# Operand tiles placed at one remainder of 256 bytes, three of them without meta columns, and weight rows of 1088 bytes

## The chip, the cores and the metric

The kernel runs on one core of one Trainium2 chip. The metric is the device time of one execution in microseconds (us). Three runs of the kernel before gave 1002.52, 1004.66 and 1006.24 us; the median is 1004.66.

## The reference

One layer of a hybrid decoder: 1024 tokens and 16 learned meta tokens ahead of them, model width 1024, float32. The normalised input goes through one wide projection whose columns feed four branches (causal pooling, latent attention with 8 heads, a Conformer convolution, a short gated convolution) and their gates; the branches are projected back, gated, added and projected once more.

```python
h = rms_norm(h_res, pre_norm_g[i])
z = h @ w_in[i]
(pv, pg, cq, ckv, kr, mg, cu, cg, sbcx, sg, gl) = split_cols(z)
...
y_b = (mla_attention(cq, ckv, kr, ...) * jax.nn.silu(mg)) @ w_out_mla[i]
...
gts = jax.nn.sigmoid(gl + gate_bias[i]).reshape(b_, l_, N_BRANCH, D_MODEL)
m = (gts[:, :, 0] * y_a + gts[:, :, 1] * y_b + gts[:, :, 2] * y_c + gts[:, :, 3] * y_d)
h_res = h_res + rms_norm(m @ w_o[i], post_norm_g[i])
...
return h_res[:, N_META:]
```

The meta tokens are dropped from the output. Their columns are needed only where later tokens look back: in the keys and values of the attention, and in the causal convolutions and pooling.

## The kernel before

**Precision.** A float32 operand is split into a high part and a rest ("hi" and "lo", `split`), and each product is three matmuls per block of 128 along the contraction: hi x hi, hi x lo, lo x hi.

**First stage, the projection.** The tokens are cut into two halves of 512 and the weights into 2x2 blocks, and a Strassen-Winograd scheme makes each 2x2 block product from seven products. The seven token operands B11, T2, T1, T3, B21, T4, B22 live in the pool `hb` at the upper end of SBUF (line 514). Each is `[128, 2, 4, n]`: the hi and the lo part, four blocks of the contraction, n columns. n is 512, or 528 with the 16 meta columns behind (`LH`), or 544 for T1 and T2; T3 and B22 have no meta columns. The seven weight blocks A11, S2, S1, S3, A12, A22, S4 are made by `prep` and `blk` in the pool `wp`, which lies behind the pools `const` and `tp` at the lower end. Each is `[128, 2, 4, 128]`, 4096 bytes a partition, from seven buffers of one tag that go round.

`unit` runs the seven products: A11 with B11, S2 with T2, S1 with T1, S3 with T3, A12 with B21, A22 with T4, S4 with B22. In the first of the pairs A12 comes right behind A11. `product` runs one of them, 12 matmuls: for each of four k the weights hi with the operand's hi, hi with lo, and lo with hi. The weights are the stationary side, the tokens stream. 23 units run with 512 columns at once; five, whose outputs need the meta tokens, run in two halves of 256 and 272 columns. Two small weight blocks (`kv`, `kr`) go through `plain` first.

The PSUM tiles tell the products apart in the profile: `ps_pa` is A11 and A12, `ps_pb` is S2 and S3, `ps_pc` is S1 and S4, `ps_pd` is A22. Buffer numbers are left out there, so that B11, B21 and B22 are all `B`, and T1 to T4 are all `T`.

**Second stage, attention** (`attend`, `maxima`): keys `kt` `[100, 2, 1040]` for even and odd heads, values `vt` `[128, 9, 192]`, queries `qt` `[100, 2, 512]`; scores `ps_s`, outputs `ps_o`. Between them run the output projections of three branches (`ps_y`).

**Third stage:** the attention's output projection and the last product with `w_o`, again by seven products; here the tokens are stationary and the weights `wa` stream.

**The order of the work.** `Plan` records every operation, and `flush` writes the order of each engine's queue out by hand from costs of its own; `Pool.lay_out` places the buffers. Each pool is a row of tags, each tag a row of equal buffers, rounded up to a multiple of 64 bytes. A buffer whose place an earlier pool held becomes free when that pool's last user ends. All weights, keys and values are loaded by SP's queue.

Of the kernel before, what the change touches and what calls it, by code (L numbers as in the profile page):

```python
# [25 lines left out]
ALU = mybir.AluOpType  # L26
# [10 lines left out]
KH = KD // 2  # L37

SBUF = 212832
H = 8  # L40
QK = 96
EPS = 1e-6
NEG = -1e30

LH = 512 + NM

C_PV, C_PG, C_CQ, C_CKV, C_KR, C_MG = 0, 256, 512, 768, 896, 928
C_CU, C_CG, C_SC, C_SG, C_GL = 1440, 1952, 2208, 2976, 3232
# [8 lines left out]
B11, B21, B22, T1, T2, T3, T4 = range(7)  # L57

B12 = T3

CH_KV = [(0, 512), (512, 512), (1024, 16)]
CH_L = [(0, 348), (348, 346), (694, 346)]
# [83 lines left out]
class Pool:  # L146
# [2 lines left out]

    def __init__(self, plan, pool, bufs=1, psum=False, side="left"):
        self.plan, self.pool, self.bufs, self.psum, self.groups = plan, pool, bufs, psum, {}
        self.space = "psum" if psum else side
        self.base = None
# [21 lines left out]
    def lay_out(self, start):  # L177

        for g in self.groups.values():
            g["one"] = -(-max(b.bytes for b in g["order"]) // 64) * 64  # L180
        size = sum(g["n"] * g["one"] for g in self.groups.values())
        at = start = start - size - SBUF % 64 if self.space == "right" else start
        for tag, g in self.groups.items():
            if not g["slots"]:
                g["slots"] = [{"i": i, "live": None, "after": 0} for i in range(g["n"])]
                for sl in g["slots"]:
                    self.pool.tile([P, g["one"] // 4], F32, tag=f"{tag}_{sl['i']}", name=f"{tag}_{sl['i']}")
            for sl in g["slots"]:
                sl["place"] = (self.space, at, at + g["one"])
                at += g["one"]  # L190
        if self.space == "right" and not self.base:
            self.base = self.pool.tile([P, SBUF % 64 // 4], F32, tag="end", name="end")
        return start if self.space == "right" else at


# [242 lines left out]
def trunk_kernel(ctx, tc, a):  # L438
# [2 lines left out]
    PE, ACT, DVE, POOL, SP = (plan.engine(e) for e in ("PE", "ACT", "DVE", "POOL", "SP"))  # L441
    ctx.enter_context(tc.manual_schedule())

    def pool(stack, **kw):
        return plan.open(stack, Pool(plan, stack.enter_context(tc.tile_pool(bufs=1, **kw)),
                                     psum=kw.get("space") == PSUM,
                                     side="dram" if kw.get("space") == DRAM else kw.get("side", "left")))

# [59 lines left out]


    one = ExitStack()  # L510
    hpool = pool(one, name="hb", side="right", reuse_waits="tile")
    HB = {}
    for b, name in ((B11, "B11"), (T2, "T2"), (T1, "T1"), (T3, "T3"), (B21, "B21"), (T4, "T4"), (B22, "B22")):
        HB[b] = hpool.tile([P, 2, KH, {T3: 512, B22: 512, T1: 544, T2: 544}.get(b, LH)], F32R, name=name)
    psum = pool(one, name="psum1", space=PSUM, reuse_waits="tile")

    def bank(tag="x"):
# [3 lines left out]
    warm = bank("w")[:, :P]  # L521
    PE.transpose(warm, ident, ident)
    tp = pool(one, name="tp", reuse_waits="tile")
    wp = pool(one, name="wp", reuse_waits="tile")
    up = pool(one, name="up", reuse_waits="tile")

    def t4(shape, dt=F32, name="t4"):
# [15 lines left out]
        return wp.tile([P, KH, 2 * P], F32, tag="raw", bufs=3, name=name)  # L543

    def blk(src, name):
        b = wp.tile([P, 2, KH, P], F32R, tag="blk", bufs=7, name=name)
        split(b[:, 0], b[:, 1], src)
        return b

    def prep(c):  # L550

# [13 lines left out]

    def product(ps, w, b, c0, n, start, stop):

        if b in (T3, B22):
            n = min(n, 512 - c0)
            ps = ps[:, :n]  # L570
        for k in range(KH):
            s = slice(c0, c0 + n)
            xh, xl = HB[b][:, 0, k, s], HB[b][:, 1, k, s]
            last = stop and k == KH - 1
            PE.matmul(ps, w[:, 0, k], xh, start=start and k == 0, stop=False, skip_group_check=True)
            PE.matmul(ps, w[:, 0, k], xl, start=False, stop=False, skip_group_check=True)
            PE.matmul(ps, w[:, 1, k], xh, start=False, stop=last, skip_group_check=True)

    EVAC = 4000

    def unit(w, c0, n, out, pump, early=False):

        pa, pb, pc, pd = (bank(t)[:, :n] for t in ("pa", "pb", "pc", "pd"))
        a_ = up.tile([P, 512], F32, tag="a", name="a_")[:, :n]
        u2 = up.tile([P, 512], F32, tag="u2", name="u2")[:, :n]
        u3 = up.tile([P, 512], F32, tag="u3", name="u3")[:, :n]  # L590

        def first():
            product(pa, w["A12"], B21, c0, n, False, True)
            with plan.ahead(EVAC):
                out(0, 0, pa, None, u3 if early else a_)
            pump()

        product(pa, w["A11"], B11, c0, n, True, True)
        with plan.ahead(EVAC):
            copy(a_, pa)  # L600
        pump()
        if early:
            first()
        product(pb, w["S2"], T2, c0, n, True, True)
        with plan.ahead(EVAC):
            add(DVE, u2, pb, a_)
        pump()
        product(pc, w["S1"], T1, c0, n, True, True)
        pump()
        product(pb, w["S3"], T3, c0, n, False, True)  # L610
        with plan.ahead(EVAC):
            add(DVE, u3, pb, a_)
            out(1, 1, pc, u3, a_)
        pump()
        if not early:
            first()
        product(pd, w["A22"], T4, c0, n, True, True)
        with plan.ahead(EVAC):
            out(1, 0, pd, u3, u3)
        pump()  # L620
        product(pc, w["S4"], B22, c0, n, False, True)
        with plan.ahead(EVAC):
            out(0, 1, pc, u2, u2)
        pump()

    def plain(w, c0, n, out):
# [78 lines left out]
    def load_x(t):  # L705

        xt[t] = (t4([P, D], name="x") if t in (4, 5, 6, 7) else
                 wp.tile([P, D], F32, tag="raw", bufs=3, name="x") if t == 0 else
                 wp.tile([P, D], F32, tag="blk", bufs=7, name="x"))
        SP.dma_start(xt[t], a["x"][0, P * t:P * (t + 1), :])  # L710
    g8 = tp.tile([KD, P], F32, tag="wraw", bufs=2, name="g8")

    with plan.slow(-2000):
        load_x(0)
        ACT.dma_start(g8, a["pre_norm_g"][0].rearrange("(k p) -> k p", p=P))
        load_x(4)
        load_x(1)
        load_x(5)
        raw_kv = [wload(i, C_CKV, P + 32) for i in range(2)]
        for t in (2, 6, 3, 7):  # L720
            load_x(t)
        xm = wp.tile([NM, D], F32, tag="blk", bufs=7, name="xm")
        SP.dma_start(xm, a["meta_tokens"])

    gC = const.tile([P, KD], F32, name="gC")
# [53 lines left out]
    def meta():  # L779
        square(xm, 8)  # L780
        rsqrt_mean(rsx[:NM, 8:9], ssx[:NM, 8:9], D)
        scaled(xm, 8)
        pt = bank()
        for k in range(KD):
            PE.transpose(pt[:, NM * k:NM * (k + 1)], xm[:, P * k:P * (k + 1)], ident[:NM, :NM])
        b1, b2 = (pt[:, 64 * i:64 * (i + 1)].rearrange("p (k n) -> p k n", n=NM) for i in range(2))
        hm = up.tile([P, 2, KH, NM], F32, tag="a", name="hm")
        copy(hm[:, 0], b1)
        sub(DVE, hm[:, 1], b2, hm[:, 0])
        for b, src, eng in ((B11, b1, DVE), (B21, b2, DVE), (T2, b1, DVE), (T4, hm[:, 1], DVE)):  # L790
            split(HB[b][:, 0, :, 512:LH], HB[b][:, 1, :, 512:LH], src, eng)
        hi = HB[T1][:, 0, :, 512:LH]
        copy(hi, b1, scale=-1.0)
        DVE.scalar_tensor_tensor(HB[T1][:, 1, :, 512:LH], b1, -1.0, f(hi), op0=ALU.mult, op1=ALU.subtract)

    rows = [
        (R_GB, 32, a["gate_bias"][0].rearrange("(k p) -> k p", p=P)),
# [16 lines left out]
        POOL.tensor_copy(t[:, :, P + 32:P + 48], t[:, :, P + 16:P + 32])  # L814
        POOL.tensor_copy(t[:, :, P + 48:P + 64], t[:, :, P:P + 16])
    w_kv = [[blk(t[:, :, :P], "kv")] for t in raw_kv]
    kr = wp.tile([P, 2, 2, KH, 64], F32R, tag="blk", bufs=7, name="kr")
    for i, t in enumerate(raw_kv):
        split(kr[:, i, 0], kr[:, i, 1], t[:, :, P:P + 64])
        w_kv[i].append(kr[:, i])  # L820
    parts(1)
    out_kv = [out_raw(("ckv", "kr"), *u) for u in (U0, U1)]
    parts(2)
# [428 lines left out]
        t.buf.group["any"] = tag == "s"  # L1252
        return t

    qk = pool(two, name="qk", reuse_waits="tile")
    fp = pool(two, name="fp", reuse_waits="tile")
    at = pool(two, name="at", reuse_waits="tile")
    cp = pool(ctx, name="cp", side="right", reuse_waits="tile")
    for d in range(4):
        cp.tag(f"mh{d}")  # L1260
    mpair = [[cp.tile([P, 2, 512], F32, name=f"m{j}{c}") for j in range(4)] for c in range(2)]
# [21 lines left out]
        ld(qt[h, c][:QK].rearrange("p s n -> p (s n)"), q_dram[c][h].rearrange("p s n -> p (s n)"))  # L1283

    load_q(0, 0)
    kt = [qk.tile([NA, 2, L], F32R, name=f"kt{i}") for i in range(2)]
    vt = [qk.tile([P, 9, 192], F32R, name=f"vt{i}") for i in range(2)]
    for i in range(2):
        POOL.memset(f(kt[i][QK:NA, 0, :]), 1.0)

    def load_kv(h):
        e, k_, v_ = h % 2, kt[h % 2], vt[h % 2]
        ld(k_[:64].rearrange("p s n -> p (s n)"), k_dram[h // 2][64 * e:64 * (e + 1)].rearrange("p s n -> p (s n)"))
        if h == 0:
            ld(k_[64:96], kr_dram)
        if h == 1:
# [210 lines left out]

    ep = pool(ctx, name="ep", reuse_waits="tile")  # L1510
    psum = pool(ctx, name="psum3", space=PSUM, reuse_waits="tile")

    def bank(tag):
# [219 lines left out]
```

## Time and profile before

| | |
|---|---|
| median of three runs | 1004.66 us |
| the profiled execution | 1002.35 us |
| its span, first to last instruction | 1000.6 us |
| granted TensorE clock, mean | 0.996 |
| DMA, mean | 203 GB/s |
| idle of TensorE in the last 10.6 us | 9.7 us |

PE is TensorE's matmuls, PEld its weight loads, DVE is VectorE, ACT ScalarE, POOL GpSimd, SP SyncE. Nearly all operations have line 332, the helper that issues them, so that groups go by tiles. A group's row gives the shape (rows * columns of the stationary side, then what streams), the count, the busy time in us, the mean ns of one, and the engine's idle time before them with what ended it. Matmuls overlap, and so a matmul's mean is longer than its share of the time; a piece of the chain of waits, divided by its count, gives the time from one start to the next.

### The profile page before, as it was taken

How to read it: one execution, taken by the hardware profiler on the slowest of the kernel's cores; microseconds unless marked ns; L12 is line 12 of the kernel's file. 1: busy time of each engine (PE TensorE's matmuls, PEld its weight loads, DVE VectorE, ACT ScalarE, POOL GpSimd, SP SyncE). 2: the span in 40 equal slices, each digit the busy share in tenths (PEclk: the TensorE clock that was granted, in tenths of full speed). 3: DMA queues.
4: the chain of work that ended last, by engine and by line, in shares of the span. 5: the costliest groups of instructions: out<-in, count | busy, mean ns of one | idle time of the engine just before them, and what ended most of it. 6: DMA issues, size and time to landing. Idle time of an engine off the chain costs nothing.

```text
span 1000.6 us, 15167 instructions
## 1 busy us (share of the span) xinstructions
PE 978.3 (98%) x5093; PEld 823.7 (82%) x5093; DVE 687.6 (69%) x1106; ACT 444.5 (44%) x895; POOL 688.9 (69%) x638
## 2 busy tenths in 40 slices
PE   9999999999999999999999999999999999999996
PEld 9999898889888887887777788877888788788885
DVE  6854794999698689553753543265777777899657
ACT  7633233344434554543543443215565656224632
POOL 6766867567776688687876865235569796656956
PEclk9999999999999999999999999999999999999998
DMA  7268756568787684786665556596757662673534
GB/s 250 76 217 281 254 173 192 187 193 256 228 272 237 217 280 146 232 252 194 183 192 174 179 172 185 203 302 182 245 160 240 195 215 93 242 242 107 187 118 168
DMA packets 126302, 203.13 MB, mean 203 GB/s; under 512 B 19650, under 2 KB 79161, under 8 KB 124880
## 3 DMA queue, kind: packets, MB, share of 16 engines
q1 hardware_dynamic: 121600, 185.38, 59.0%
q10 hardware_dynamic: 4336, 15.73, 4.2%
q8 instruction: 40, 0.66, 0.3%
q0 software_dynamic: 288, 1.05, 0.3%
q14 instruction: 38, 0.31, 0.1%
HBM read 128.40 MB, written 73.72 MB: 202 GB/s over the span
## 4 chain that ended last, share of the span: by engine, by line
PE 84%; DVE 6%; POOL 4%; issue 3%; DMA 2%; ACT 0%; SPq 0%; DVEq 0%; POOLq 0%; ACTq 0%
PE ps_pb L332 14%; PE ps_pa L332 14%; PE ps_pc L332 13%; PE ps_o L332 10%; PE ps_u L332 7%; PE ps_s L332 7%; PE ps_y L332 7%; PE ps_pd L332 6%; PE ps_x L332 4%; DVE ps_w L332 2%; PE ps_w L332 1%; DMA raw<-in_w_in_dram 1%; DVE ss L332 1%; DMA kt<-kr 1%; POOL S L332 1%
## 5 line engine op out<-in xcount | busy, mean ns | idle before, releaser
L332 PE MATMUL ps_pb<-T,S 128*128 128x512 f32 (+2 forms) x792 | 173.8, 362 | 0.7 <-DVE u L332 0.7
L332 PE MATMUL ps_pa<-B,A 128*128 128x512 f32 (+2 forms) x792 | 172.7, 363 | 0.0
L332 POOL TENSOR_TENSOR S<-ss,S 128x512 fp32r<-128x512 f32 x84 | 113.7, 1367 | 70.0 <-ACT S L332 69.0
L332 PEld LDWEIGHTS ps_pa<-B,A 128*128 128x128 f32 x792 | 134.5, 188 | 24.3 <-issue 0.5
L332 PEld LDWEIGHTS ps_pb<-T,S 128*128 128x128 f32 x792 | 133.7, 188 | 24.8 <-issue 0.7
L332 POOL TENSOR_TENSOR A<-raw,A 128x512 fp32r<-128x512 f32 x84 | 115.5, 1382 | 43.5 <-ACT A L332 41.2
L332 POOL TENSOR_TENSOR pt<-p,pt 128x512 fp32r<-128x512 f32 (+4 forms) x112 | 102.3, 939 | 47.6 <-PE ps_s L332 30.0
L332 DVE SCALAR_TENSOR_TENSOR ps_w<-conv,par,ps_w 128x512 f32<-128x512 f32 x116 | 87.2, 751 | 2.4
L332 PE MATMUL ps_pc<-T,S 128*128 128x512 f32 (+2 forms) x396 | 87.0, 363 | 0.0
L332 PE MATMUL ps_pc<-B,S 128*128 128x512 f32 (+1 forms) x396 | 85.5, 361 | 0.5 <-DVE z L332 0.5
L332 PE MATMUL ps_pd<-T,A 128*128 128x512 f32 (+2 forms) x396 | 85.8, 361 | 0.0
L332 ACT ACTIVATE S<-ss 128x512 fp32r<-128x512 f32 x84 | 50.8, 628 | 72.4 <-DVE ss L332 38.3
L332 ACT ACTIVATE p<-ps_s 128x512 f32<-128x512 f32 (+4 forms) x112 | 49.6, 442 | 73.3 <-PE ps_s L332 29.2
L332 PE MATMUL ps_y<-bo,whl 128*128 128x512 f32 x288 | 81.8, 403 | 0.3 <-DVE op L332 0.3
L332 PEld LDWEIGHTS ps_pc<-B,S 128*128 128x128 f32 x396 | 67.0, 188 | 13.2 <-DVE z L332 0.7
L332 PEld LDWEIGHTS ps_pd<-T,A 128*128 128x128 f32 x396 | 67.3, 188 | 12.1
L332 PEld LDWEIGHTS ps_pc<-T,S 128*128 128x128 f32 x396 | 66.9, 188 | 12.2 <-issue 0.7
L332 PE MATMUL ps_o<-pt,vt 128*128 128x512 f32 (+4 forms) x336 | 74.5, 334 | 2.0 <-ACT ol L332 1.6
L332 PE MATMUL ps_s<-qt,kt 100*128 100x512 f32 (+4 forms) x336 | 67.0, 325 | 0.7 <-DVE qt L332 0.7
L332 PEld LDWEIGHTS ps_o<-pt,vt 128*128 128x128 f32 (+1 forms) x336 | 52.9, 173 | 15.8 <-ACT ol L332 3.2
L332 ACT ACTIVATE A<-raw 128x512 fp32r<-128x512 f32 x84 | 52.4, 625 | 28.4 <-PE ps_pd L332 14.6
L332 PEld LDWEIGHTS ps_s<-qt,kt 100*128 100x128 f32 (+1 forms) x336 | 54.1, 176 | 11.1 <-issue 0.9
(342 smaller groups left out, 1893.0 us busy)
## 6 DMA issues: line engine op xcount, KB each, us to landing
raw<-in_w_in_dram SPq DMA_DIRECT2D x56, 512.0 KB
th<-th SPq DMA_DIRECT2D x32, 512.0 KB
th<-z ACTq DMA_DIRECT2D x30, 512.0 KB
v<-vhl SPq DMA_DIRECT2D x16, 384.0 KB
qt<-q SPq DMA_DIRECT2D x16, 384.0 KB
vt<-v SPq DMA_DIRECT2D x8, 768.0 KB
bo<-bo SPq DMA_DIRECT2D x6, 1024.0 KB
kt<-k SPq DMA_DIRECT2D x8, 520.0 KB
```

The source lines that it names most:

```text
L332: getattr(self.handle[o["eng"]], o["op"])(*map(real, o["args"]), **{k: real(v) for k, v in o["kw"].items()})
```

## The change

It does five things.

- Pools can have a `grain`. In `hb`, `wp`, `qk`, `fp`, `at`, `cp` and `ep` it is 256: tags over 256 bytes are rounded up to multiples of 256, come first, and the pool starts at a remainder of `PLACE` = 64 by 256. The pools `const`, `tp` and `up` keep 64.
- T1 loses its meta columns and joins T3 and B22 (`BARE`, 512 columns); T2 has 528 columns instead of 544. The two operations that made T1's meta columns go, and S1's product with T1 streams at most 512 - c0 columns, so that the outputs from `ps_pc` are cut to `nb`.
- A weight block is `[128, 4, 256]`: in each row the hi part and behind it the lo part, rows of 1024 bytes.
- The blocks A11, S2, A12 and A22 (`SKEW`) have 16 columns more in each row, rows of 1088 bytes. They have a tag of their own with four buffers, and the other blocks one with three.
- The keys' rows are 1088 columns (`LK`) instead of 1040, of which 1040 are used; they are loaded as two runs per partition.

```diff
+PLACE = 64
+LK = 1088
+BARE = (T1, T3, B22)
+SKEW = ("A11", "S2", "A12", "A22")
...
     def lay_out(self, start):
         for g in self.groups.values():
-            g["one"] = -(-max(b.bytes for b in g["order"]) // 64) * 64
-        size = sum(g["n"] * g["one"] for g in self.groups.values())
-        at = start = start - size - SBUF % 64 if self.space == "right" else start
-        for tag, g in self.groups.items():
+            one = max(b.bytes for b in g["order"])
+            grain = self.grain if one > 256 else 64
+            g["one"] = -(-one // grain) * grain
+        groups = sorted(self.groups.items(), key=lambda x: self.grain > 64 and x[1]["one"] <= 256)
+        size = sum(g["n"] * g["one"] for _, g in groups)
+        if self.space == "right":
+            gap = (start - PLACE) % self.grain
+            at = start = start - size - gap
+        else:
+            gap = (PLACE - start) % self.grain if self.space == "left" else 0
+            at = start + gap
...
-        HB[b] = hpool.tile([P, 2, KH, {T3: 512, B22: 512, T1: 544, T2: 544}.get(b, LH)], F32R, name=name)
+        HB[b] = hpool.tile([P, 2, KH, 512 if b in BARE else LH], F32R, name=name)
...
     def blk(src, name):
-        b = wp.tile([P, 2, KH, P], F32R, tag="blk", bufs=7, name=name)
-        split(b[:, 0], b[:, 1], src)
-        return b
+        skew = name in SKEW
+        b = wp.tile([P, KH, 2 * P + 16 * skew], F32R, tag="blks" if skew else "blk", bufs=3 + skew, name=name)
+        hi, lo = b[:, :, :P], b[:, :, P:2 * P]
+        split(hi, lo, src)
+        return hi, lo
...
-        pa, pb, pc, pd = (bank(t)[:, :n] for t in ("pa", "pb", "pc", "pd"))
+        nb = min(n, 512 - c0)
+        pa, pb, pc, pd = (bank(t)[:, :m] for t, m in (("pa", n), ("pb", n), ("pc", nb), ("pd", n)))
...
-        hi = HB[T1][:, 0, :, 512:LH]
-        copy(hi, b1, scale=-1.0)
-        DVE.scalar_tensor_tensor(HB[T1][:, 1, :, 512:LH], b1, -1.0, f(hi), op0=ALU.mult, op1=ALU.subtract)
...
-    kt = [qk.tile([NA, 2, L], F32R, name=f"kt{i}") for i in range(2)]
+    kt = [qk.tile([NA, 2, LK], F32R, name=f"kt{i}") for i in range(2)]
...
-        ld(k_[:64].rearrange("p s n -> p (s n)"), k_dram[h // 2][64 * e:64 * (e + 1)].rearrange("p s n -> p (s n)"))
+        k_ = k_[:, :, :L]
+        ld(k_[:64], k_dram[h // 2][64 * e:64 * (e + 1)])
```

More of the change, by code (lines that the diff above doesn't have):

```diff
@@ L146, with __init__ @@
 class Pool:
-    def __init__(self, plan, pool, bufs=1, psum=False, side="left"):
+    def __init__(self, plan, pool, bufs=1, psum=False, side="left", grain=64):
+        self.grain = grain
         self.plan, self.pool, self.bufs, self.psum, self.groups = plan, pool, bufs, psum, {}
@@ L179, in lay_out @@
         for g in self.groups.values():
-            g["one"] = -(-max(b.bytes for b in g["order"]) // 64) * 64
-        size = sum(g["n"] * g["one"] for g in self.groups.values())
-        at = start = start - size - SBUF % 64 if self.space == "right" else start
-        for tag, g in self.groups.items():
+            one = max(b.bytes for b in g["order"])
[9 more added lines that the diff above has]
+            at = start + gap
+        if gap and not self.base and self.space == "left":
+            self.base = self.pool.tile([P, gap // 4], F32, tag="gap", name="gap")
+        for tag, g in groups:
             if not g["slots"]:
@@ L190, in lay_out @@
                 at += g["one"]
-        if self.space == "right" and not self.base:
-            self.base = self.pool.tile([P, SBUF % 64 // 4], F32, tag="end", name="end")
+        if gap and not self.base:
+            self.base = self.pool.tile([P, gap // 4], F32, tag="gap", name="gap")
         return start if self.space == "right" else at
@@ L442, in trunk_kernel, with pool @@
     ctx.enter_context(tc.manual_schedule())
-    def pool(stack, **kw):
-        return plan.open(stack, Pool(plan, stack.enter_context(tc.tile_pool(bufs=1, **kw)),
+    def pool(stack, grain=64, **kw):
+        return plan.open(stack, Pool(plan, stack.enter_context(tc.tile_pool(bufs=1, **kw)), grain=grain,
                                      psum=kw.get("space") == PSUM,
@@ L510, in trunk_kernel @@
     one = ExitStack()
-    hpool = pool(one, name="hb", side="right", reuse_waits="tile")
+    hpool = pool(one, 256, name="hb", side="right", reuse_waits="tile")
     HB = {}
     for b, name in ((B11, "B11"), (T2, "T2"), (T1, "T1"), (T3, "T3"), (B21, "B21"), (T4, "T4"), (B22, "B22")):
-        HB[b] = hpool.tile([P, 2, KH, {T3: 512, B22: 512, T1: 544, T2: 544}.get(b, LH)], F32R, name=name)
+        HB[b] = hpool.tile([P, 2, KH, 512 if b in BARE else LH], F32R, name=name)
     psum = pool(one, name="psum1", space=PSUM, reuse_waits="tile")
@@ L523, in trunk_kernel @@
     tp = pool(one, name="tp", reuse_waits="tile")
-    wp = pool(one, name="wp", reuse_waits="tile")
+    wp = pool(one, 256, name="wp", reuse_waits="tile")
     up = pool(one, name="up", reuse_waits="tile")
@@ L566, in product @@
     def product(ps, w, b, c0, n, start, stop):
-        if b in (T3, B22):
+        if b in BARE:
             n = min(n, 512 - c0)
@@ L574, in product @@
             last = stop and k == KH - 1
-            PE.matmul(ps, w[:, 0, k], xh, start=start and k == 0, stop=False, skip_group_check=True)
-            PE.matmul(ps, w[:, 0, k], xl, start=False, stop=False, skip_group_check=True)
-            PE.matmul(ps, w[:, 1, k], xh, start=False, stop=last, skip_group_check=True)
+            PE.matmul(ps, w[0][:, k], xh, start=start and k == 0, stop=False, skip_group_check=True)
+            PE.matmul(ps, w[0][:, k], xl, start=False, stop=False, skip_group_check=True)
+            PE.matmul(ps, w[1][:, k], xh, start=False, stop=last, skip_group_check=True)
     EVAC = 4000
     def unit(w, c0, n, out, pump, early=False):
-        pa, pb, pc, pd = (bank(t)[:, :n] for t in ("pa", "pb", "pc", "pd"))
+        nb = min(n, 512 - c0)
+        pa, pb, pc, pd = (bank(t)[:, :m] for t, m in (("pa", n), ("pb", n), ("pc", nb), ("pd", n)))
         a_ = up.tile([P, 512], F32, tag="a", name="a_")[:, :n]
@@ L612, in unit @@
             add(DVE, u3, pb, a_)
-            out(1, 1, pc, u3, a_)
+            out(1, 1, pc, u3[:, :nb], a_)
         pump()
@@ L622, in unit @@
         with plan.ahead(EVAC):
-            out(0, 1, pc, u2, u2)
+            out(0, 1, pc, u2[:, :nb], u2)
         pump()
@@ L708, in load_x @@
                  wp.tile([P, D], F32, tag="raw", bufs=3, name="x") if t == 0 else
-                 wp.tile([P, D], F32, tag="blk", bufs=7, name="x"))
+                 wp.tile([P, D], F32, tag="blks", bufs=4, name="x"))
         SP.dma_start(xt[t], a["x"][0, P * t:P * (t + 1), :])
@@ L721, in trunk_kernel @@
             load_x(t)
-        xm = wp.tile([NM, D], F32, tag="blk", bufs=7, name="xm")
+        xm = wp.tile([NM, D], F32, tag="blks", bufs=4, name="xm")
         SP.dma_start(xm, a["meta_tokens"])
@@ L816, in trunk_kernel @@
     w_kv = [[blk(t[:, :, :P], "kv")] for t in raw_kv]
-    kr = wp.tile([P, 2, 2, KH, 64], F32R, tag="blk", bufs=7, name="kr")
+    kr = wp.tile([P, 2, 2, KH, 64], F32R, tag="blk", bufs=3, name="kr")
     for i, t in enumerate(raw_kv):
         split(kr[:, i, 0], kr[:, i, 1], t[:, :, P:P + 64])
-        w_kv[i].append(kr[:, i])
+        w_kv[i].append((kr[:, i, 0], kr[:, i, 1]))
     parts(1)
@@ L1253, in bank @@
         return t
[L1255 to L1258, printed above, removed]
+    qk = pool(two, 256, name="qk", reuse_waits="tile")
+    fp = pool(two, 256, name="fp", reuse_waits="tile")
+    at = pool(two, 256, name="at", reuse_waits="tile")
+    cp = pool(ctx, 256, name="cp", side="right", reuse_waits="tile")
     for d in range(4):
@@ L1285, in trunk_kernel @@
     load_q(0, 0)
-    kt = [qk.tile([NA, 2, L], F32R, name=f"kt{i}") for i in range(2)]
+    kt = [qk.tile([NA, 2, LK], F32R, name=f"kt{i}") for i in range(2)]
     vt = [qk.tile([P, 9, 192], F32R, name=f"vt{i}") for i in range(2)]
     for i in range(2):
-        POOL.memset(f(kt[i][QK:NA, 0, :]), 1.0)
+        POOL.memset(f(kt[i][QK:NA, 0, :L]), 1.0)
     def load_kv(h):
         e, k_, v_ = h % 2, kt[h % 2], vt[h % 2]
-        ld(k_[:64].rearrange("p s n -> p (s n)"), k_dram[h // 2][64 * e:64 * (e + 1)].rearrange("p s n -> p (s n)"))
+        k_ = k_[:, :, :L]
+        ld(k_[:64], k_dram[h // 2][64 * e:64 * (e + 1)])
         if h == 0:
@@ L1505, in trunk_kernel @@
     two.close()
-    ep = pool(ctx, name="ep", reuse_waits="tile")
+    ep = pool(ctx, 256, name="ep", reuse_waits="tile")
     psum = pool(ctx, name="psum3", space=PSUM, reuse_waits="tile")
```

## The prediction

> **What bounds the kernel now.** I read the page first (busy shares, clock, chain), then the pieces of the chain of waits in order of time, then the groups by shape of TensorE, then the waits.
>
> ```profile
> span 1000.6 us, 15167 instructions
> PE 978.3 (98%) x5093; PEld 823.7 (82%) x5093; DVE 687.6 (69%) x1106; ACT 444.5 (44%) x895; POOL 688.9 (69%) x638
> PEclk9999999999999999999999999999999999999998
> PE 84%; DVE 6%; POOL 4%; issue 3%; DMA 2%; ACT 0%; SPq 0%; DVEq 0%; POOLq 0%; ACTq 0%
> ```
>
> TensorE is busy 98% of the span at a full granted clock, and it carries 84% of the chain. Only fewer or faster matmuls shorten this program. So the question is what one matmul costs and on what that depends. One whole weight unit of the projection stage stands in the chain like this (start, length, tile, matmuls):
>
> ```profile
> 595.96 2.80 PE ps_pa L332 x12
> 598.75 2.79 PE ps_pb L332 x12
> 601.54 2.79 PE ps_pc L332 x12
> 604.33 2.78 PE ps_pb L332 x12
> 607.11 2.80 PE ps_pa L332 x12
> 609.91 2.78 PE ps_pd L332 x12
> 612.69 2.78 PE ps_pc L332 x12
> ```
>
> The order is that of `unit`: A11, S2, S1, S3, A12, A22, S4. The seven pieces add up to 19.52 us for 84 matmuls, 232.4 ns each, with no gap. Now matmuls of the same shape (128x512) elsewhere: the first pieces of the last stage, two blocks of it later, an attention stretch of `ps_s` alone (head 0), and one of `ps_y` alone.
>
> ```profile
> 871.01 4.39 PE ps_u L332 x19
> 875.17 4.99 PE ps_u L332 x22
> 914.62 21.76 PE ps_o L332 x96
> 936.38 21.76 PE ps_u L332 x96
> 683.27 2.57 PE ps_s L332 x11
> 655.88 10.26 PE ps_y L332 x45
> ```
>
> That is 231.1 ns for the first 19 of the last stage, 226.8 for the next 22, 226.7 for 96 in a row, 233.6 for `ps_s`, 228.0 for `ps_y`. The same instruction thus has two prices, 232 and 226.7, and the low one is reached after some twenty matmuls. What differs is where the operands lie. I added up the tile sizes in bytes from the planner's zero and took the rest by 256. In the last stage `wa`, `mh` and `boM` all lie at 64, and all steps inside them are multiples of 512. In the projections the operand tiles start at 94528 (SBUF 212832, less 32, less their 118272), rest 64; the weight pool starts at 39104, rest 192. `kt0` starts at 16704, rest 64, but its low half 4160 bytes on, rest 128. The next weights are loaded while the matmul before still streams:
>
> ```profile
> 605.79 1.32 PE L332 MATMUL ps_pb<-T,S 128*128 128x512 f32 x5
> 606.72 0.89 PEld L332 LDWEIGHTS ps_pa<-B,A 128*128 128x128 f32 x4
> 606.95 0.87 PE L332 MATMUL ps_pa<-B,A 128*128 128x512 f32 x3
> ```
>
> The load for `ps_pa` starts at 606.72, inside the streams of `ps_pb` that last until 607.11. So what counts is the rest of the next weights less that of the running stream; I call it the offset. It is 0 throughout the last stage. For S3 and S4 it is a constant 128 now, and 2.78/12 = 231.7 ns shows that a constant offset is not enough: it has to be 0. For `kt0` it is 0, 64, 0 in every three matmuls (high rows again, low rows, the next high rows), and the price is 233.6: two loads of three in phase buy nothing.
>
> The Trainium skill says otherwise: by "TensorE: Matmul & The Clock Gate" (Step-by-step: what each phase is for) TensorE has two independent read ports, and loading the next weights takes no read bandwidth from the running matmul. By that rule placement would change nothing, and the sum below would shrink to its shorter T1 streams. The 232.4 against 226.7 ns above speaks against it, though these rows alone do not exclude another difference between the stages.
>
> **The change part by part.** Durations by shape:
>
> ```profile
> L332 PE MATMUL ps_pb<-T,S 128*128 128x512 f32 x552 | 139.9, 395 | 0.2 <-DVE u L332 0.2
> L332 PE MATMUL ps_pa<-B,A 128*128 128x512 f32 x552 | 138.6, 396 | 0.0
> L332 PE MATMUL ps_y<-bo,whl 128*128 128x512 f32 x288 | 81.8, 403 | 0.3 <-DVE op L332 0.3
> L332 PE MATMUL ps_o<-wa,mh 128*128 128x512 f32 x192 | 43.8, 389 | 0.0
> L332 PE MATMUL ps_s<-qt,kt 96*128 96x512 f32 x96 | 31.0, 395 | 0.0
> L332 PE MATMUL ps_s<-qt,kt 100*128 100x512 f32 x48 | 19.3, 402 | 0.7 <-DVE qt L332 0.7
> L332 PE MATMUL ps_o<-pt,vt 128*128 128x512 f32 x96 | 35.7, 403 | 2.0 <-ACT ol L332 1.6 <-POOL pt L332 0.2 <-ACT pt L332 0.2
> L332 PE MATMUL ps_pb<-T,S 128*128 128x256 f32 x180 | 24.2, 282 | 0.4 <-DVE u L332 0.4
> L332 PE MATMUL ps_pc<-B,S 128*128 128x256 f32 x120 | 16.2, 283 | 0.5 <-DVE z L332 0.5
> L332 PE MATMUL ps_pc<-T,S 128*128 128x272 f32 x60 | 8.5, 290 | 0.0
> L332 PE MATMUL ps_pc<-T,S 128*128 128x256 f32 x60 | 7.9, 281 | 0.0
> L332 PE MATMUL ps_o<-wa,B 128*128 128x256 f32 x12 | 1.6, 283 | 0.0
> ```
>
> These durations overlap, so I use only their differences; 389 is the settled price, and 395 to 396 the projections' now. 552 matmuls of `ps_pa` are 23 full units of two blocks of 12, so 23 x 84 = 1932 matmuls.
>
> *S1, S3, S4* (36 of 84): the weight pool moves to rest 64, and T1, T3, B22 and these blocks have rows that are multiples of 256, so the offset is 0. They come as 24 in a row (S1, S3) and 12 (S4), between blocks of the other kind. Settling like the last stage (19 at 231.1, then 226.8) against 232.0 now (8.35/36): 24 x 232.0 - 19 x 231.1 - 5 x 226.8 = 43 ns, and 12 x 0.9 = 11 ns; 54 ns x 23 = **-1.2 us**. Bounds: 0, and -4.3 if all settle at once (36 x 23 x 5.2 ns).
>
> *A11, S2, A12, A22* (48 of 84): their operands (T2 now too) have rows of 2112 bytes, which step the rest by 64, and the new rows of 1088 step with them. Inside one k the offset is 0; but the load behind the third matmul is that of the next k, 64 ahead. That is the pattern 0, 0, 64, which `kt0` has today at 233.6. Now they cost 232.7 ((2.80 + 2.79 + 2.80 + 2.78)/48). So +0.9 x 1104 = **+1.0 us**. Bounds: 226.8 gives -6.5; the dearest shape above, 402 against some 395.5 now, gives +7.2.
>
> *T1 without meta columns*: 60 matmuls stream 256 instead of 272 columns, 290 - 281 = 9 ns each, **-0.5 us**. One activation and one VectorE operation of 128x64 go as well, at the start:
>
> ```profile
> L332 ACT ACTIVATE T<-ps_x 128x64 fp32r<-128x64 f32 x2 | 0.5, 228 | 0.7 <-PE ps_x L332 0.7
> L332 DVE SCALAR_TENSOR_TENSOR T<-ps_x,T 128x64 fp32r<-128x64 f32 x1 | 0.2, 224 | 0.7 <-ACT B L332 0.7
> ```
>
> I cost them at nothing, since the matmuls of the first projection (`ps_pa<-B,kv`) run beside them; if those waited for them, the change would gain up to 0.228 + 0.224 = 0.45 us more.
>
> *Half-width S streams*: settled 256-column matmuls take 283, these 281 to 283 now; the five units with meta columns run in two halves, so 6 blocks x 12 x 5 x 1 ns = **+0.4 us** (0 to +0.7).
>
> *Attention*: rows of `kt` become 4352 bytes and both `kt` start at 64, so all three offsets of `ps_s` are 0, as they are for `ps_o` and `ps_y`. At most (395 - 389) x 96 + (402 - 389) x 48 = 1.2 us for full-width `ps_s`, and as much again for the 144 narrower ones; 432 `ps_y` and `ps_o` between them at 5 ns, 2.2. At least nothing, since the three kinds alternate in threes and never run nineteen alike. I take a third, **-1.5 us**.
>
> *Queues, other pools, order*: the last stage is at offset 0 already, so moving its pools is worth 0. `kt` is loaded in two runs per partition, behind other loads of the same queue:
>
> ```profile
> 668.87 8.91 DMA kt<-kr
> PE ps_s L332 <- DMA kt<-kr: 2.3, 1, 2.3
> ```
>
> This is TensorE's longest wait. A microsecond more of landing time would be a microsecond more of wait. The planner's costs change with T1's width, the block tags split 7 into 4 and 3 (each name still follows its own predecessor), and the layouts at the stage borders shift by some hundred bytes. I take 0 and allow 1.5 either way.
>
> Sum: -1.2 + 1.0 - 0.5 + 0.4 - 1.5 = **-1.8 us**. The profiled execution took 1002.35 us (span 1000.6 and 1.75 around it), 2.3 below the median of 1004.66. I set the base between them at 1003.5: **1001.7 us**.
>
> **The rivals.** *Everything settles* (0.30): the step of 64 is made by operand and weights together, so it may not break the phase. For it: inside each k the offset is 0. Against it: `kt0`. Then 1932 x (232.4 - 226.8) = 10.8, and the T1, half-width and attention terms, 1.6 more: -12.4, about 991. *The 1088-byte rows are dearer* (0.12): one load in three 64 ahead falls into a costlier cycle, as the 100-row `ps_s` at 402 shows is possible; at the upper bound +7.2 - 1.2 - 0.5 + 0.4 = +5.9, 1009.4. It outweighs all gains once A blocks cost over 1.8 + 1.0 = 2.8 us more, 2.5 ns a matmul. *Placement does nothing* (0.08), the two prices having another cause: T1 alone, 1003.0.
>
> **How the numbers follow.** My forecast has 0.50, its own range 997.5 to 1006 from the bounds of S, attention and order. A measurement of this kernel tells about 0.5%, 5 us, from no change. Faster by that: the first rival's 0.30 and 0.15 of the forecast (S near its bound, attention in full): 0.45. Slower: most of the second rival and a little for an order that breaks, 0.12. Within: 0.43. The range for 8 in 10 takes in most of the first rival and part of the second: 990 to 1008.
>
> **What would show it.** In the chain, pieces of `ps_pc` and `ps_pb` after S1 and S3 of 2.72 to 2.78 us instead of 2.79, and durations near 389 in `ps_pc<-T,S`; `ps_pa` and `ps_pd` at 2.79 to 2.81. If `ps_pa` falls to 2.72, the first rival is right; above 2.83, the second; if `ps_pc` stays at 395 to 397, the third. `ps_s` should fall below 395. The wait for `kt<-kr` shows the loads. It would be wrong above all if the phase holds over the step of 64.

## The result, and the profile after

The kernel after takes 993.37 us (median of 4 runs, 992.87 to 994.93), the kernel before beside it 1005.04 (4 runs, 1002.52 to 1006.24): a ratio of 0.9878, 95% interval 0.9859 to 0.9896, so 11.7 us or 1.2% faster. The forecast was 1001.7, 1.8 below its base. The sign and the range held; the size did not, and most of it came from a place that the prediction had put at nothing.

The chain of waits of the kernel after, by engine:

```profile
PE 92%; DVE 4%; DMA 2%; issue 1%; POOL 1%; ACT 0%; SPq 0%; DVEq 0%; POOLq 0%; ACTq 0%
```

This profiled execution took 994.93 us, the longest of its four; that of before, with 1002.35, was the shortest of its runs. So the two traces differ by 7.4 us where the medians differ by 11.7: 2.7 more lies between the trace of before and its median (1005.04 - 1002.35), 1.6 between the trace of after and its own. What the chain shows first is that TensorE carries 92% of it instead of 84%, while DVE and POOL fall from 10% to 5%: waits of TensorE have gone.

The chain of waits after, one whole weight unit (start, length, tile, matmuls), in the order A11, S2, S1, S3, A12, A22, S4:

```profile
604.42 2.76 PE ps_pa L350 x12
607.17 2.78 PE ps_pb L350 x12
609.95 2.74 PE ps_pc L350 x12
612.70 2.72 PE ps_pb L350 x12
615.42 2.76 PE ps_pa L350 x12
618.17 2.78 PE ps_pd L350 x12
620.95 2.74 PE ps_pc L350 x12
```

Together 19.28 us against 19.52. S1, S3 and S4 lost 0.15 us a unit, and A11, S2, A12 and A22 lost 0.09, where the prediction had -0.054 and +0.04.

Groups by shape after:

```profile
L350 PE MATMUL ps_pa<-B,A 128*128 128x512 f32 x552 | 139.6, 395 | 0.0
L350 PE MATMUL ps_pb<-T,S 128*128 128x512 f32 x552 | 137.8, 392 | 0.0
L350 PE MATMUL ps_pc<-T,S 128*128 128x512 f32 x276 | 68.1, 393 | 0.0
L350 PE MATMUL ps_s<-qt,kt 96*128 96x512 f32 x96 | 31.2, 396 | 0.0
```

`ps_pb` fell from 395 to 392, `ps_pa` from 396 to 395; `ps_s` did not fall at all (395 before).

The borders of the stages in the chain after: the long piece of `ps_y` with which attention begins, the load that TensorE waits for, an undisturbed piece of `ps_s`, and the last block of `ps_u`:

```profile
644.36 10.26 PE ps_y L350 x45
657.77 11.76 DMA kt<-kr
675.09 2.58 PE ps_s L350 x11
929.11 21.76 PE ps_u L350 x96
```

Before, the first stood at 655.88 and the last at 936.38. So the projections end **11.5 us** earlier, and 4.2 us of that are lost again up to that last block (936.38 - 929.11 = 7.3 are left).

The waits of TensorE in the first 640 us, of the kernel before (releaser: total, times, longest):

```profile
PE ps_x L332 <- POOL rs L332: 1.5, 2, 1.1
PE ps_x L332 <- DVE rs L332: 1.1, 1, 1.1
PE ps_y L332 <- DVE pd L332: 0.8, 1, 0.8
PE ps_pb L332 <- DVE u L332: 0.7, 2, 0.4
PE ps_pc L332 <- DVE z L332: 0.5, 1, 0.5
```

and all that are listed for the kernel after:

```profile
PE ps_w L350 <- POOL conv L350: 1.4, 1, 1.4
PE ps_x L350 <- DVE rs L350: 0.4, 1, 0.4
```

`ps_w<-conv` stands at the start of both. The others of before, 5.5 us with four short ones that are not shown, are gone but for 0.4. They are waits for VectorE and GpSimd, one short one for ScalarE; that byte addresses set them is not likely, and the experiments test it. The planner had written another order: TensorE's queue departs from that of before at its 290th matmul, transposes counted. That gives two theories. **P**: the gain is the price of a matmul by the place of its operands. **O**: it is the planner's other order.

### The profile page after: what moved, and what is told of

Read it like the earlier page. It is cut to its first block, busy times and chain, and to the rows that moved or that the text cites. A ratio compares the mean times of both kernels' runs of the same rounds, so it can differ in the third digit from the quotient of the medians.

```text
span 993.2 us, 15194 instructions
## 1 busy us (share of the span) xinstructions
PE 971.4 (98%) x5093; PEld 823.4 (83%) x5093; DVE 691.2 (70%) x1105; ACT 446.4 (45%) x894; POOL 693.7 (70%) x638
## 4 chain that ended last, share of the span: by engine, by line
PE 92%; DVE 4%; DMA 2%; issue 1%; POOL 1%; ACT 0%; SPq 0%; DVEq 0%; POOLq 0%; ACTq 0%
PE ps_pa L350 16%; PE ps_pb L350 16%; PE ps_pc L350 15%; PE ps_o L350 10%; PE ps_pd L350 7%; PE ps_s L350 7%; PE ps_y L350 7%; PE ps_u L350 7%; PE ps_x L350 4%; PE ps_w L350 1%; DMA kt<-kr 1%; DVE ps_w L350 1%; DVE op L350 1%; DVE a L350 0%; DVE m L350 0%
## 5 line engine op out<-in xcount | busy, mean ns | idle before, releaser
L350 PE MATMUL ps_pb<-T,S 128*128 128x512 f32 (+2 forms) x792 | 170.9, 359 | 0.0
L350 POOL TENSOR_TENSOR S<-ss,S 128x512 fp32r<-128x512 f32 x84 | 117.5, 1411 | 61.1 <-ACT S L350 60.8
L350 POOL TENSOR_TENSOR A<-raw,A 128x512 fp32r<-128x512 f32 x84 | 118.3, 1415 | 50.2 <-ACT A L350 45.1
L350 PE MATMUL ps_pc<-T,S 128*128 128x512 f32 (+1 forms) x396 | 84.2, 359 | 0.0
L350 PEld LDWEIGHTS ps_pd<-T,A 128*128 128x128 f32 x396 | 67.3, 188 | 11.7
L350 PEld LDWEIGHTS ps_pc<-B,S 128*128 128x128 f32 x396 | 66.9, 188 | 11.7 <-issue 0.5
L350 PEld LDWEIGHTS ps_pc<-T,S 128*128 128x128 f32 x396 | 66.7, 188 | 11.7 <-issue 0.5
```

Of the source, the lines that this page charges most:

```text
L350: getattr(self.handle[o["eng"]], o["op"])(*map(real, o["args"]), **{k: real(v) for k, v in o["kw"].items()})
```

## The experiments

### P and O apart

`e1_pool_moved`: the kernel before, with one tile more ahead of the weight pool; the order of instructions is that of before.

```diff
+    wp.tile([P, 32], name="pad")
```

> The kernel before with one added tile of 128 bytes ahead of the weight pool, and the same instructions in the same order. S3 and S4 meet T3 and B22 at offset 0; the other five products still meet operands whose rows step the offset. Theory P (the price of a matmul hangs on the offset): the pieces of ps_pb after S3 and of ps_pc after S4 fall from 2.78 to 2.72 to 2.74 us, 0.08 to 0.12 us a unit, so 2 to 3 us less than before (ratio 0.997 to 0.998), and the idle gaps of TensorE in the projections stay. Theory O (the gain came from the planner's other order of instructions): within 1 us of before, pieces unchanged at 2.78.

1004.04 us (median of 10), ratio 0.9987 (0.9971 to 1.0004). In the chain S3 and S4, the start of the attention stage, and the last block of `ps_u`:

```profile
603.40 2.77 PE ps_pb L332 x12
611.74 2.74 PE ps_pc L332 x12
654.72 10.26 PE ps_y L332 x45
937.80 21.76 PE ps_u L332 x96
```

S4 meets the expectation, S3 hardly (2.78 to 2.77). Both stand between products whose operands step. T1, ahead of S3, steps by 128 bytes, and T4, ahead of S4, by 64; `e7_meta_kept` below shows the same pair, 2.77 and 2.74, but no run takes the cause apart. The stage ends 1.2 us earlier (655.88 - 654.72), and its gaps of over 100 ns add up as before. Placement has an effect, and in the old order it is small; in the time alone it is not clear of noise.

The trace shows one thing more. The attention stage, whose order is that of before, takes 283.1 us here (654.72 to 937.80) and took 280.5 in the trace of before (655.88 to 936.38). The load of `kt` ends at 677.7 and 677.8, so that the wait for it grows from 2.3 to 3.4 us, by what the projections gained, and TensorE's clock stands at half for 6.8 us behind it instead of 3.4. The trace of before is also not a usual one: its mean clock is 0.996, like that of one run of before beside this one (1002.44 us), while the other 13 have 0.990 to 0.993.

`e3_out_of_phase`: the kernel after, with the weights 128 bytes off every operand.

```diff
-            gap = (PLACE - start) % self.grain if self.space == "left" else 0
+            gap = (PLACE + getattr(self, "off", 0) - start) % self.grain if self.space == "left" else 0
...
+    wp.off = 128
```

> The kernel after with the weight pool alone put back by 128 bytes, so that every block starts 128 off its operand; the same instructions in the same order as after. Theory P: the pieces of a unit go back to 2.78 to 2.80 us, 19.5 us a unit, so some 5.5 us slower than after, 998.5 to 999.5. Theory O: 993 to 994.5, as after. If both take part: 5 us slower than after and still 5 to 6 us faster than before.

997.21 us (median of 4, 993.44 to 998.52), ratio 0.9915 (0.9884 to 0.9946). The chain: A11, S1, S3, and the start of attention:

```profile
606.48 2.80 PE ps_pa L350 x12
612.08 2.79 PE ps_pc L350 x12
614.87 2.80 PE ps_pb L350 x12
646.99 10.29 PE ps_y L350 x45
```

TensorE's queue is that of the kernel after, matmul by matmul. Not one product is cheaper than before, and yet the stage ends 8.9 us earlier than before's 655.88. That is O, plus T1's shorter streams, which both kernels of this order have. From 646.99 to 644.36 (and 643.36 in a second trace of the kernel after) there remain 2.6 to 3.6 us for P. Both take part, and O is the larger.

`e2_no_skew`: the kernel after with all blocks in rows of 1024 bytes.

```diff
-        b = wp.tile([P, KH, 2 * P + 16 * skew], F32R, ...
+        b = wp.tile([P, KH, 2 * P], F32R, ...
```

> The kernel after with the blocks A11, S2, A12 and A22 in rows of 1024 bytes again, the same instructions in the same order. Theory P with the prediction's working (one load of three 64 ahead is as bad as any): no difference to after, within 0.1%. Theory P with a price by how many loads are in phase: pa, pb after S2 and pd rise from 2.76 to 2.78 us to 2.79 to 2.80, 0.08 us a unit, 1.5 to 2.5 us slower than after. Theory O: same as after.

996.10 us (median of 5, 991.45 to 998.32), ratio 0.9904 (0.9871 to 0.9937). The chain: A11, S1, S3, and the start of attention:

```profile
605.77 2.79 PE ps_pa L350 x12
611.34 2.74 PE ps_pc L350 x12
614.08 2.72 PE ps_pb L350 x12
645.84 10.26 PE ps_y L350 x45
```

The rows of 1088 bytes take A11 and A12 from 2.79 to 2.76. Adding up, in each trace, the times from the start of one product matmul to that of the next up to the attention stage (2,697 to 2,699 of them, gaps over 100 ns left out) gives 538.0 us before, 536.4 for the moved pool, and in the new order 536.2 out of phase, 533.9 with rows of 1024, 531.9 after. The traces of `e8_after_again`, `e10_keys_early` and `e12_old_keys`, with the same projections as after, give 531.9 too. So the phase of S1, S3 and S4 is worth about 2.3 us (A11 and A12 hardly differ between the first two, 2.80 and 2.79), and the longer rows about 2.0, 4.3 together. The times alone do not part this run from after: the intervals of their ratios overlap.

### What the price of a matmul hangs on

`e5_streams` runs streams of 72 matmuls alone, one PSUM tile each, in one execution.

> Computes none of the reference: streams of 72 matmuls 128x512 with nothing else beside them, one PSUM tile each, at offsets that are set by hand (a, b, c, d: constant 0, 64, 128, 192). Theory P: ps_consta 226.7 ns a matmul from some point on, ps_constb, c and d about 232; ps_keys (0, 64, 0 with a fixed stream, as kt0 before) near 233; ps_follow (the 0, 0, 64 of the A blocks after) between, 229 to 231; ps_lag (the low rows 64 bytes behind, products low-high, high-high, high-low, so that every offset is 0) 226.7; ps_rowsall and ps_rowsmix (offset 0 with 96, and with 100, 96, 96 rows) 226.7 if the rows do not matter, about 233 if they are why ps_s did not gain. The rival, that another thing than the offset tells the stages apart: all 72-matmul streams the same within 1 ns.

Its chain (start, length, tile, matmuls):

```profile
20.61 16.32 PE ps_consta L37 x72
36.93 16.80 PE ps_constb L37 x72
53.73 16.72 PE ps_constc L37 x72
70.45 16.48 PE ps_constd L37 x72
86.93 16.63 PE ps_keys L37 x72
103.56 16.67 PE ps_follow L37 x72
136.95 16.67 PE ps_lag L37 x72
153.62 16.36 PE ps_rowsall L37 x72
169.98 16.80 PE ps_rowsmix L37 x72
```

By 72 that is 226.7 ns at offset 0, and 233.3, 232.2 and 228.9 at 64, 128 and 192: nothing else differs between these four, so the offset alone makes the price. Four rows were not foreseen. `ps_constd`, at 192, costs 228.9 and not about 232. `ps_keys`, the 0, 64, 0 of `kt0`, costs 231.0 and not the 233.6 of `ps_s`. `ps_rowsmix` is at offset 0 throughout and costs 233.3, where 100 and 96 rows alternate; with 96 alone (`ps_rowsall`) it is 227.2. Its addresses also move to and fro by 2048 bytes, but such steps cost nothing in `ps_nostep` below (226.7). And `ps_lag` has offset 0 for every load, but its streams move on by 64 bytes after every third matmul: 231.5. My offset was not the whole condition. Either a step of the streams themselves costs too, or it counts as well that one block of three starts 192 bytes off its own stream there; this run does not tell the two apart.

`e9_unit_streams` runs the seven products of a unit twice in each arrangement.

> Computes none of the reference: the seven products of one unit, 84 matmuls 128x512, twice in a row for each arrangement, with nothing else beside them. If the offset alone sets the price, the second unit of each costs what the units in the kernels cost: straight (every block 128 off) 19.5 us, plain (all bases in phase, rows of 1024) 19.35, skew (rows of 1088) 19.28, nostep (operand rows of 2048 bytes) 84 x 226.7 ns = 19.04. Each step of 64 in the streams is then worth (19.28 - 19.04)/16 = 15 ns, so turn (S2 and A22 go through k from 3 to 0, 12 steps instead of 16) should give 19.22, and skewdown (all four from 3 to 0) anything between. If other work beside the matmuls raised the price in the kernels, all arrangements come out below those numbers by the same amount.

```profile
34.69 38.40 PE ps_straight L44 x165
73.09 38.47 PE ps_plain L44 x167
150.20 38.56 PE ps_skew L44 x168
227.43 38.51 PE ps_turn L44 x168
343.21 38.08 PE ps_nostep L44 x168
```

Per matmul 232.7, 230.4, 229.5, 229.2 and 226.7 ns; the four arrangements not shown lie between 229.5 and 230.5. The undisturbed units of the kernels cost the same as the arrangement with their rows: 19.34/84 = 230.2 in `e2_no_skew` (`ps_plain`) and 19.28/84 = 229.5 after (`ps_skew`). So nothing that runs beside them adds to the price. Turning S2 and A22 round gives 0.025 us a unit, not the 0.06 expected.

The Trainium skill, "TensorE: Matmul & The Clock Gate" (Step-by-step: what each phase is for), has two independent read ports, by which a load of weights takes nothing from the running matmul. The row of `ps_nostep` against that of `ps_straight` disagrees: 226.7 against 232.7 ns, with only addresses changed.

### What made the order better

`e6_one_tag` is the kernel of `e2_no_skew` with one tag of seven buffers, for the weight blocks and for the input tiles that use the same buffers at the start.

```diff
-        b = wp.tile(..., tag="blks" if skew else "blk", bufs=3 + skew, name=name)
+        b = wp.tile(..., tag="blk", bufs=7, name=name)
```

> The kernel after with all weight blocks in rows of 1024 bytes and in one tag of seven buffers as before; placement at rest 64 and T1 without meta columns stay. To be compared with the run whose blocks lie in rows of 1024 bytes in two tags. If the split into two tags is what made the planner's order better: the six idle gaps of TensorE in the projections (at z, u, rs, rs, rs and pd; 4.3 us together before) come back, and it is 3 to 5 us slower than that run, near 1000. If T1's two operations or the placement did it: no gaps, 995 to 997.

1005.09 us (median of 12), ratio 0.9987 (0.9974 to 0.9999). Its waits, and the start of attention:

```profile
PE ps_x L350 <- DVE rs L350: 1.1, 1, 1.1
PE ps_x L350 <- POOL rs L350: 1.0, 2, 0.7
PE ps_s L350 <- DVE mr L350: 2.8, 1, 2.8
```

```profile
649.16 10.26 PE ps_y L350 x45
```

Four of the six named gaps are back (those at `rs`, `rs`, `rs` and `z`); gaps of over 100 ns, without the first one at `conv`, add up to 3.1 us in the projections instead of 0.4, and the stage ends 3.3 us later (649.16 - 645.84). The attention's order differs too: it has a new wait of 2.8 us for `mr`, where `e2_no_skew` has 0.2, and from its start to the last block of `ps_u` it takes 290.0 us (to 939.13) instead of 283.9 (645.84 to 929.72). The undisturbed units are as cheap as in `e2_no_skew`, 19.34 us, and yet nearly the whole gain is gone: 3.3 us in the projections and 6.1 in attention.

`e7_meta_kept` is the kernel of `e2_no_skew` with T1's meta columns and their two operations.

```diff
-BARE = (T1, T3, B22)
+BARE = (T3, B22)
```

> The kernel after with all weight blocks in rows of 1024 bytes and with T1's meta columns and their two operations as before; the two tags stay. T1 and T2 then have rows of 2176 bytes, so S1 and S2 step by 128. If T1's operations are what changed the order for the better: the gaps come back, near 1000. If the split of the tags did it: no gaps; S1 back at 2.78 to 2.79 us a piece (0.04 x 23 = 1 us), 0.5 us of wider streams, so 1 to 2 us slower than the run with rows of 1024 bytes.

1002.02 us (median of 6), ratio 0.9955 (0.9941 to 0.9970). One gap of 0.8 us at `rs` and two short ones at the start come back, 1.3 us in all, and the stage ends 2.1 us later:

```profile
647.97 10.26 PE ps_y L350 x45
```

Not all of that is order: S1 and S3 take 2.79 and 2.77 us again, where `e2_no_skew` has 2.74 and 2.72, with T1's rows stepping by 128 bytes again. It too has the wait of 2.8 us for `mr`, and its attention takes 287.2 us (to 935.13), so that in all it is over 5 us longer than `e2_no_skew`, more than either expectation. So the split of the tags removes some 2.7 us of gaps in the projections (3.1 - 0.4) and T1's operations some 0.9 (1.3 - 0.4), and either one alone leaves a dearer order in attention. That the order came with these two parts of the change is shown; why the planner makes the better one from them is not.

### The attention stage

`e8_after_again` is the kernel after, unchanged.

> The kernel after, unchanged, beside the others of this call: 992 to 995 us, with the same gaps of TensorE as its first trace, and the wait for kt<-kr anywhere between 3.3 and 5.5 us, since the three kernels with its order showed 5.5, 3.3 and 3.5.

993.89 us (median of 4), ratio 0.9877 (0.9861 to 0.9893); the wait for `kt<-kr` 3.4 us. TensorE's granted clock (the third number from the end) in windows of 4 us, before, around its wait of 2.3 us that ended at 677.9:

```profile
676.00:680.00 4.00, 2.08 (x8) 2.00 (x9) 1.54 (x6) 0.00 (x1) 0.96 (x4) 0.75 0.95 262
680.00:684.00 4.00, 4.00 (x21) 3.40 (x20) 1.90 (x5) 0.60 (x1) 0.00 (x0) 0.82 0.16 47
```

and in this run, whose wait ended at 666.5:

```profile
664.00:668.00 4.00, 1.49 (x6) 1.41 (x7) 1.08 (x5) 0.00 (x0) 0.46 (x3) 0.50 1.01 279
668.00:672.00 4.00, 4.00 (x17) 3.53 (x17) 0.93 (x2) 0.60 (x1) 0.00 (x0) 0.50 0.25 69
672.00:676.00 4.00, 4.00 (x15) 3.17 (x14) 3.31 (x9) 1.46 (x3) 0.10 (x1) 0.75 0.07 13
```

The wait began at 663.1. Shorter windows of the same trace show the clock at 0.50 from 663.8 to 674.0, so that half clock lasted 10.2 us and ended 7.5 us behind the wait. In the trace of before it lasted 3.4 us, from 678.0 to 681.4, in the first of after 6.8. So a wait of a few microseconds is paid for beyond its length, by an amount that differs between executions of one kernel.

`e10_keys_early` is the kernel after with the second head's keys and values asked for ahead.

```diff
     load_kv(0)
     load_q(*seq[1])
+    load_kv(1)
...
-            if c == 0 and h + 1 < H:
+            if c == 0 and 0 < h < H - 1:
```

> The kernel after with the loads of the second head's keys and values recorded ahead of the first head's work instead of inside it, so that they stand ahead of the first weights and gates of the output projections in SP's queue; the projections are untouched. If the wait for kt<-kr is a matter of the queue's order: the wait of 3.4 to 5.5 us goes, and with it the stretch of half clock that followed it (0.50, 0.50 and 0.75 in three windows of 4 us), 4 to 7 us, 987 to 990. If the transfers of that stretch as a whole are the bound (the DMA share is near 1.0 from 652 to 668 us): another load comes late instead (whl or th for ps_y), and the time stays within 1.5 us of after.

993.26 us (median of 5, 990.65 to 994.82), ratio 0.9874 (0.9855 to 0.9893): the same as after. The wait for `kt<-kr` and the half clock behind it are gone (1.00 in every window from 648 to 680 us). From the start of attention to the last block of `ps_u` it takes 282.1 us (642.77 to 924.84) instead of 284.4 in `e8_after_again` (643.36 to 927.72). In place of it `ps_y` waits at the stage's end:

```profile
PE ps_y L350 <- DVE th L350: 2.2, 2, 1.6
```

The clock falls there too: 0.72 and 0.86 in the windows of 4 us from 856 to 864. The second expectation came nearer: a load was moved ahead, and something else is late.

`e11_turn` is `e10_keys_early` with the turned products.

```diff
-        for k in range(KH):
+        ks = range(KH)[::-1] if b in (T2, T4) else range(KH)
+        for k in ks:
```

> As the run before, and the products S2 and A22 go through k from 3 to 0, so that their streams begin where A11 and A12 ended (12 steps of 64 a unit instead of 16). By the streams measured alone (38.56 us for two units without, 38.51 with) 0.025 x 23 = 0.6 us less than the run before, with S2 and A22 at 2.76 instead of 2.78 and S1 and S4 at 2.74 or below. If the other work beside the matmuls sets these pieces: no difference.

991.02 us (median of 4, 990.93 to 992.77), ratio 0.9861 (0.9844 to 0.9878). S2 and A22 stand at 2.77 instead of 2.78, so the effect of the turn is smaller than expected. All its runs lie below all eight of the kernel after (992.87 to 995.40). But it has the early keys as well, and next to `e10_keys_early` nothing is gained: its runs lie inside the range of that one (990.65 to 994.82), and its product matmuls, added up as above, take 532.0 us against 531.9. That the turn helps a whole kernel is not shown.

`e12_old_keys` is the kernel after with `LK = 1040` and one run per partition for the keys.

> The kernel after with the keys' rows of 1040 columns and their load in one run per partition, as before; the projections keep the order and the places of after, the attention's order differs. By the prediction's term: ps_s at 128x512 and its narrower kinds dearer by up to 1.5 us. If the change of rows (100 and 96 in turn) keeps ps_s from settling anyway, as the streams alone showed with 233.3 ns at offset 0: pieces of ps_s as in after within 1 ns a matmul, and what moves is only the wait for kt<-kr (2.3 to 5.5 us in either).

994.01 us (median of 4, 991.11 to 995.07), ratio 0.9878 (0.9854 to 0.9902), as after. The same undisturbed piece of 11 `ps_s` takes 2.78 us (at 695.35) and 2.80 after (at 695.10): the keys' rows change nothing, and the wait for `kt<-kr` is 3.4 us here too.

## Why the prediction was wrong in size

- **Queues, other pools, order: 0 +-1.5.** This step failed. "Each name still follows its own predecessor" looked at the buffers and not at what the planner makes of them. `e3_out_of_phase`, with every product out of phase, ends the projections 8.9 us earlier than before. Of these 5.2 are gaps of over 100 ns (5.5 to 0.3), about 0.4 are T1's, and the rest lies in products and small matmuls interleaved in another way, which no run took apart further.
- **S1, S3, S4: -1.2.** Right in mechanism, but the forecast is half of what came: about 2.3 us. What failed is "settling like the last stage", after 19 matmuls: S1 needs 2.74 us, 0.02 more than 12 settled matmuls (12 x 226.7 ns = 2.72), and S3 behind it not even that. Why the last stage's first 19 cost 231.1 stays open. The bound of -4.3 held.
- **A11, S2, A12, A22: +1.0.** Wrong in sign: about -2.0 us in the kernels, 0.9 ns a matmul over a whole unit in the streams (230.4 to 229.5). I took the price of 0, 0, 64 from `kt0`, but 100 and 96 rows in turn cost as much at offset 0 (`ps_rowsmix` 233.3), and its offsets without them cost less (`ps_keys` 231.0). A row gave the price of something else that differed in it.
- **Attention: -1.5.** Nothing, for the same reason: `ps_s` is 395 and 396, and an undisturbed piece takes 2.57 and 2.58 us. Between the two traces the stage gave 4.2 us back: the wait for `kt<-kr` is 5.5 us instead of 2.3, `ps_o` waits 2.4 instead of 1.6 for `ol`, and half clock comes with the wait. The load had moved ahead less than the projections: it ended 8.3 us earlier (677.8 to 669.5), they 11.5. That is not peculiar to the new order: in the order of before `e1_pool_moved` took 283.1 us for the stage, with a wait of 3.4, and after took 284.7 and 284.4, the second time with 3.4 as well. Against a usual run of before the stage thus loses nearer to 1.5 us than to 4.2; this is an estimate from these traces.
- **T1 (-0.5) and the half-width streams (+0.4).** T1's streams are 282 ns now and were 288 in `e7_meta_kept`, 0.4 us over 60. The half-width ones are at 279 to 282, not dearer. Alone, 72 matmuls of 256 columns take 8.64 us at offset 0 and 8.54 at 128 (`ps_halfa` and `ps_halfc` of `e5_streams`), so at this width the offset buys nothing. Both terms were too small to matter.
- **The rivals.** "Everything settles" gives a time near the measured one, but is not what happened: `ps_pa` is 2.76 and not 2.72, and the step of 64 does break the phase (`ps_follow` 231.5). The dearer rows are refuted by `e2_no_skew`. That placement does nothing is refuted by `e5_streams`. The forecast's own range, 997.5 to 1006, missed; that the wide one held is luck, since it reached down to 990 for the first rival and not for another order.

By terms the trace reads: order and T1 -8.9, placement -2.6 at the end of the projections (4.3 in the products' own times; the other matmuls, transposes at the start above all, took 1.6 longer in this trace than in that of `e3_out_of_phase`), attention +4.2, sum -7.3. The medians lie 4.4 us further apart. The 2.6 us that the attention of `e1_pool_moved` takes longer than in the trace of before, and the 1.0 by which the projections end earlier in the second trace of after (643.36), come near to that; as single traces stand for medians here, this is an estimate.

## What to carry to other kernels

Where a planner orders the work by hand, a change of buffers is a change of order first: compare the order of the queues and the idle gaps before pricing anything else, and keep the order fixed when the effect of an address is to be measured. A price read from another stage holds only if every difference to that stage is known; a stream by itself, with one thing changed, costs one run. A late load can cost more than its wait, since the clock fell with it here and stayed low behind it; a stage with such a wait needs more than one trace.

## What the hardware showed that was not expected

- Matmuls 128x512 in float32 cost 226.7 ns when the next weights and the running stream start at the same remainder by 256 bytes, 233.3, 232.2 and 228.9 when they differ by 64, 128 and 192 (`e5_streams`); in streams that step by 64 the low price was not reached even where each load agreed (231.5). Matmuls 128x256 cost 120.0 ns at the same remainder and 118.6 at 128.
- Stationary sides of 100 and 96 rows in turn cost 233.3 ns where 96 alone cost 227.2, at the same remainders.
- In a wait of 3.4 us that began at 663.1 TensorE's granted clock fell to 0.50 at 663.8 and stayed there to 674.0 us (`e8_after_again`). The Trainium skill, "TensorE: Matmul & The Clock Gate" (Part 1: The HAM clock gate (the "warmup" mystery)), gives half clock after an idle window of about 3.4 us and full clock after as long a busy one. The level agrees; here it fell within 1 us of the wait's start, in a window of 4 us in which TensorE was busy for 2.86 and the wait itself took 0.9, and it took 7.5 us of work to come back. The wait of 2.3 us before brought half clock from 678.0 to 681.4.
